# Loading x once, token-major, and turning it on the array, with low-rank products by token block

## The chip, the cores and the metric

One core of a Trainium2 chip runs the whole program. The metric is the device time of one execution in microseconds (us). The core has a matrix engine (PE, with its weight loads, PEld, shown apart), VectorE (DVE), ScalarE (ACT), GpSimd (POOL) and a queue engine (SP) that only issues DMAs here; ACT also issues some.

## The reference

A two-layer decoder trunk on 512 tokens of width 1024, all in float32. Layer 0 is an RWKV-7 time mix, layer 1 a differential attention; only the head of layer 0 matters here:

```python
xn = rms_norm(h, norm_pre[i])
x_prev = jnp.pad(xn, ((0, 0), (1, 0), (0, 0)))[:, :-1]
xmix = xn[None] + (x_prev - xn)[None] * mu[:, None, None, :]
rkvg = jnp.einsum('cbsd,cde->cbse', xmix[:4], w_in)
xw, xa = xmix[4], xmix[5]
w_pre = (w0 + jnp.tanh(xw @ w1) @ w2).astype(f32)
a = jax.nn.sigmoid((a0 + (xa @ a1) @ a2).astype(f32))
```

So x is normalised per token, multiplied by a gain per channel, and mixed with the token before it six times, with six vectors mu: four mixes go into products with 1024x1024 weights (r, k, v, g), two into low-rank products of width 64 (w1 and a1, side by side 128 columns).

## The kernel before

**Work and tiles.** Channels lie on the 128 partitions in 8 tiles (d = 0 to 7), tokens in 4 blocks of 128 (tb). A large product is split into high and low float32r parts and made of three matmuls of 512 columns (`mm3`, L284 to L287). `fill` (L909) walks the weight halves in the order r0, k0, v0, r1, k1, v1, ... (`ORDER`, L35); for each, `dense_m` (L396) needs for every d the split weight (`w_split`, L304) and the mixed activation (`mix`, `mixed`, L512 to L531), and then issues 4 x 3 matmuls.

**Order.** Each part of the work is a generator that yields its engine and an estimated cost. A planner (`Streams`, L45) runs them at build time: it always takes the step that can start earliest by its own clock, and among equals the one with the lower priority number. The instruction order of PE, DVE, ACT and POOL is the order in which the planner took the steps, and each engine runs its list in order. Buffers are counted: 4 PSUM banks for products (`pd`) and 4 for the rest (`pw`), 8 split weights (`WT`), 2 raw weights (`RAW`), 2 mixed tiles for even d and 2 for odd d (`MT`).

**The head.** `x_load` (L435) loads, on SP's queue and in this order: the vectors `vec`, the low-rank weights `w1a1`, two quarters of a channel-major copy of x (`xT`), the identity, the four token blocks of x, and the other two quarters of `xT`. All these pieces of x and `w1a1` have 512 KB. `x_in` (L462) squares a token block on ACT, takes the root on POOL (`rsqrt`, L275) and scales the identity with it (L474); `x_norm` (L477) turns the four diagonal matrices into one row of norms on every partition by four matmuls with ones (L492) and an ACT copy (L494). `lora_w` (L565) multiplies the low-rank weights with the mixing vectors, half on DVE and half on POOL (L573). `lora` (L580) makes the low-rank products of the still unnormalised x, 2 x 8 matmuls of 512 columns (L589, L590); `lora_out` (L595) multiplies both results with the norms (L600, L602) and adds them one token apart (L605). `x_scale` (L499) multiplies each channel tile with gain and norms (L504), and only then may `mixed` run on it: ACT L519, DVE L521, ACT L523 and DVE L525. The priorities are 0 for `x_load`, `x_in`, `lora_w` and `lora`, 6 for `x_scale`, 4 and 5 for the mixes, 7 for the weight splits, and 8 for `fill`. `w_split` waits until the norms are there. `r_evac` (L670) empties r's banks, and `decay` (L742) builds the decays from them and from the low-rank results (PE L749, L750).

Of the kernel before, what the change touches and what calls it, by code (L numbers as in the profile page):

```python
# [202 lines left out]
def yoco_kernel(ctx: ExitStack, tc: tile.TileContext, I, out):  # L203
# [58 lines left out]
    vec = cload("vec", [P, NVEC, NT])  # L262
# [41 lines left out]
    def w_split():  # L304
        yield "wait", ("norms",)
# [126 lines left out]
    xt, dg = [None] * NB, [None] * NB  # L432
    xh, norm, w1a1 = [], [], []

    def x_load():  # L435

        yield "DMA!", 0.2
        yield "set", ("vec",)
        for n in ("w", 0, 1, "x", 2, 3):
            if n == "w":  # L440
                yield "take", "R", 2
                w1a1.extend(R([P, NT, P]) for _ in range(2))
                yield "DMA!", 1.46
                nc.sync.dma_start(w1a1[0], I["w1a1"])
                yield "set", ("w1a1",)
            elif n == "x":
                yield "DMA!", 0.2
                nc.sync.dma_start(ident, I["ident"])
                for tb in range(NB):
                    yield "take", "R", 1  # L450
                    xt[tb] = R([P, D])
                    yield "DMA!", 1.46
                    nc.sync.dma_start(xt[tb], I["x"][tb])
                    yield "set", ("x", tb)
            else:
                yield "take", "R", 1
                xh.append(R([P, 2, S]))
                yield "DMA!", 1.46
                nc.sync.dma_start(xh[n], I["xT"][n])
                yield "set", ("xT", n)  # L460

    def x_in(tb):  # L462
        yield "wait", ("x", tb)
# [3 lines left out]
        yield "ACT", 1.04  # L467
        nc.scalar.activation(sq, xt[tb], AF.Square, accum_out=ss)
        yield "free", "R", 2
        r = yield from rsqrt(small, ss, 1.0 / D, EPS, 1, "rs")  # L470
        yield "take", "H", 1
        dg[tb] = HT([P, P])
        yield "DVE+", 0.15
        nc.vector.tensor_scalar(dg[tb], ident, r, None, ALU.mult)  # L474
        yield "set", ("dg", tb)

    def x_norm():  # L477

        ones = T(ax, [P, P], "ones")
        yield "Pool!", 0.1  # L480
        nc.gpsimd.memset(ones, 1.0)
        yield "take", "H", 1
        yield "take", "pw", 1
        nrm = bank("pw")
        n_ = HT([P, S])
        norm.append(n_)
        for tb in range(NB):
            yield "wait", ("dg", tb)
        yield "PE", 0.86
        for tb in range(NB):  # L490
            sl = slice(tb * P, (tb + 1) * P)
            nc.tensor.matmul(nrm[:, sl], ones, dg[tb], start=True, stop=True)  # L492
        yield "ACT", 0.52
        nc.scalar.copy(n_, nrm)  # L494
        yield "set", ("norms",)
        yield "free", "H", 4
        yield "free", "pw", 1

    def x_scale():  # L499
        yield "wait", ("norms",)  # L500
        for d in range(NT):
            yield "wait", ("low", d)
            yield "DVE+!", 0.66
            nc.vector.scalar_tensor_tensor(x_at(d), x_at(d), vcol(V_G, d), norm[0], ALU.mult, ALU.mult)  # L504
            yield "set", ("xh", d)
# [6 lines left out]
    def mixed(key, d, t):  # L512
# [8 lines left out]
        nc.vector.scalar_tensor_tensor(m[:, 1:], x_at(d)[:, 0 : S - 1], vcol(V_MU + c, d), m[:, 1:], ALU.mult, ALU.add)  # L521
# [58 lines left out]
    def lora():  # L580
# [4 lines left out]
        for d in range(NT):  # L585
            yield "wait", ("w1", d // 4)
            yield "wait", ("xT", d // 2)
            yield "PE", 1.71
            nc.tensor.matmul(ps, w1[:, d, :], x_at(d), start=(d == 0), stop=(d == NT - 1))  # L589
            nc.tensor.matmul(pm, m1[:, d, :], x_at(d), start=(d == 0), stop=(d == NT - 1))  # L590
            yield "set", ("low", d)
# [1392 lines left out]
```

## Time and profile before

| | |
|---|---|
| median of 3 runs | 792.98 us (791.94 to 794.04) |
| the profiled execution, its time | 797.09 us |
| the profiled execution, its span | 795.3 us |
| mean granted clock of PE over the span | 0.989 |
| instructions | 13941 |

The profile is that of one execution. A row of the timeline gives the start, the time that the merged instructions take together, engine, line, operation, written and read tile, a count, and in brackets the idle time before and what ended it. The end of a matmul is modelled and overlaps the next one's start, so the pace of PE is read from start to start. One f32 matmul of the low-rank products is two records.

### The profile page before, as it was taken

What the parts mean: (1) busy time and instruction counts of PE and PEld (TensorE: products, weight loads), DVE (VectorE), ACT (ScalarE), POOL (GpSimd) and SP (SyncE); (2) the same over time, 40 slices, a digit from 0 to 9 for tenths busy, and PEclk for the clock granted to TensorE, in tenths of its full rate; (3) what the DMA queues carried; (4) which work ended last, traced back from release to release, by engine and by line L of the source; (5) the groups of instructions that cost most, each with busy time, mean ns of one, the idle gap of its engine ahead of it and who ended that gap; (6) DMA issues with size and microseconds to landing.
All of it is one profiled execution on the core that took longest, in us unless ns stands there. A gap on an engine that the chain in (4) does not pass through costs nothing.

```text
span 795.3 us, 13941 instructions
## 1 busy us (share of the span) xinstructions
PE 756.1 (95%) x5016; PEld 605.1 (76%) x5016; DVE 589.8 (74%) x1360; ACT 454.5 (57%) x1078; POOL 201.9 (25%) x221
## 2 busy tenths in 40 slices
PE   6899999998999899999989999999999999999996
PEld 3576578875777677777778888887888888888884
DVE  2989999976798898998676685446874768835844
ACT  3779745688875446664444564333764566743431
POOL 2416615521451425666010010000000001100000
PEclk9999999998999899999999999999999999999998
DMA  8585669843684687463446444488943523314602
GB/s 325 197 285 196 245 225 290 298 147 105 209 286 171 217 301 258 145 228 105 133 166 247 133 146 135 172 309 226 312 158 92 159 53 121 117 43 159 259 6 106
DMA packets 66677, 148.79 MB, mean 187 GB/s; under 512 B 6576, under 2 KB 27312, under 8 KB 66608
## 3 DMA queue, kind: packets, MB, share of 16 engines
q1 hardware_dynamic: 43824, 112.25, 41.9%
q10 hardware_dynamic: 22784, 35.66, 13.1%
q8 instruction: 39, 0.64, 0.3%
q14 instruction: 30, 0.25, 0.1%
HBM read 110.13 MB, written 37.75 MB: 186 GB/s over the span
## 4 chain that ended last, share of the span: by engine, by line
PE 70%; DVE 8%; ACT 8%; DMA 8%; issue 2%; POOL 2%; SPq 1%; ACTq 0%; POOLq 0%; DVEq 0%
PE p L285 18%; PE p L287 18%; PE p L286 18%; PE p L1788 2%; PE p L984 2%; PE p L1188 2%; ACT R L270 1%; PE p L1753 1%; PE p L1752 1%; PE p L1201 1%; DMA R<-bD 1%; PE p L1779 1%; DMA RAW<-in_ple_w 1%; PE p L1410 1%; DMA R<-mD 1%
## 5 line engine op out<-in xcount | busy, mean ns | idle before, releaser
L285 PE MATMUL p<-R,R 128*128 128x512 f32 x800 | 326.4, 408 | 3.2 <-DVE R L270 1.7
L286 PE MATMUL p<-R,R 128*128 128x512 f32 x800 | 314.1, 393 | 3.8 <-DVE R L525 3.6
L287 PE MATMUL p<-R,R 128*128 128x512 f32 x800 | 314.4, 393 | 0.0
L285 PEld LDWEIGHTS p<-R,R 128*128 128x128 f32 x800 | 151.3, 189 | 37.1 <-DVE R L270 1.9
L287 PEld LDWEIGHTS p<-R,R 128*128 128x128 f32 x800 | 151.0, 189 | 33.2 <-DVE R L1318 0.4
L286 PEld LDWEIGHTS p<-R,R 128*128 128x128 f32 x800 | 151.5, 189 | 32.4 <-DVE R L525 4.9
L318 POOL TENSOR_TENSOR R<-RAW,R 128x512 fp32r<-128x512 f32 x59 | 78.6, 1339 | 163.3 <-ACT R L270 89.1
L270 ACT CAST R<-RAW 128x512 fp32r<-128x512 f32 x110 | 66.1, 619 | 26.7 <-DMA RAW<-in_w_g 10.0
L318 DVE TENSOR_TENSOR R<-RAW,R 128x512 fp32r<-128x512 f32 x81 | 56.8, 715 | 11.0 <-ACT R L270 10.2
L324 DVE SCALAR_TENSOR_TENSOR R<-RAW,vec,R 128x512 fp32r<-128x512 f32 x64 | 46.6, 748 | 13.9 <-ACT R L322 13.7
L322 ACT ACTIVATE R<-RAW,vec 128x512 fp32r<-128x512 f32 x64 | 44.6, 720 | 17.0 <-DMA RAW<-in_b_w_in 9.1
L1397 POOL TENSOR_TENSOR hr<-hm,half 128x1 f32<-128x1 f32 x16 | 10.4, 648 | 147.2 <-DVE hm L1395 147.2
L1757 DVE CUSTOM_DVE_ANT_0 p<-p,cmask 128x128 f32<-128x128 f32 (+3 forms) x64 | 30.3, 509 | 17.4 <-PE p L1753 17.3
L1764 ACT ACTIVATE H<-p,mx 128x128 f32<-128x128 f32 (+3 forms) x64 | 33.3, 526 | 15.7 <-DVE mx L1761 14.1
L281 POOL TENSOR_TENSOR orr<-orm,half 128x4 f32<-128x4 f32 x8 | 8.4, 1055 | 123.3 <-DVE orm L279 93.3
L1054 DVE TENSOR_TENSOR p<-p,H 128x126 f32<-128x126 f32 (+22 forms) x124 | 32.6, 263 | 4.3
L1051 DVE TENSOR_TENSOR H<-p,R 128x126 f32<-128x126 f32 (+22 forms) x124 | 30.5, 246 | 1.1
L1534 DVE SCALAR_TENSOR_TENSOR R<-H,R 128x512 f32<-128x512 f32 x16 | 11.1, 691 | 24.5 <-ACT H L1527 23.1
L1527 ACT ACTIVATE H<-p 128x512 f32<-128x512 f32 x16 | 9.5, 596 | 31.6 <-PE p L287 31.6
L521 DVE SCALAR_TENSOR_TENSOR p<-R,vec,p 128x511 f32<-128x511 f32 x32 | 23.5, 747 | 5.4 <-ACT p L519 5.3
L519 ACT ACTIVATE p<-R,omm 128x512 f32<-128x512 f32 x32 | 22.0, 695 | 5.0 <-DVE R L525 3.7
L1788 PEld LDWEIGHTS p<-R,H 128*128 128x128 f32 x160 | 22.1, 191 | 2.8 <-ACT H L1805 0.5
(227 smaller groups left out, 1249.4 us busy)
## 6 DMA issues: line engine op xcount, KB each, us to landing
R<-mD SPq DMA_DIRECT2D x40, 512.0 KB, 5.3
mD<-R ACTq DMA_DIRECT2D x32, 512.0 KB, 4.3
RAW<-in_ple_gate SPq DMA_DIRECT2D x16, 512.0 KB, 3.7
RAW<-in_kv_w SPq DMA_DIRECT2D x16, 512.0 KB, 3.9
RAW<-in_b_w_in SPq DMA_DIRECT2D x16, 512.0 KB, 3.9
R<-bD ACTq DMA_DIRECT2D x24, 256.0 KB, 5.2
R<-in_x SPq DMA_DIRECT2D x8, 512.0 KB, 6.8
RAW<-in_w_r SPq DMA_DIRECT2D x8, 512.0 KB, 4.0
```

The costliest lines, as they stand in the source:

```text
L270: (nc.scalar.copy if sc.eng == "ACT" else ENG[sc.eng].tensor_copy)(dst, src)
L285: nc.tensor.matmul(ps, ah, bh, start=first, stop=False)
L286: nc.tensor.matmul(ps, ah, bl, start=False, stop=False)
L287: nc.tensor.matmul(ps, al, bh, start=False, stop=last)
L318: ENG[sc.eng].tensor_sub(lo, f, hi.bitcast(F32))
L322: nc.scalar.activation(hi, f, AF.Copy, scale=g)
L324: nc.vector.scalar_tensor_tensor(lo, f, g, hi.bitcast(F32), ALU.mult, ALU.subtract)
L1051: ve.tensor_mul(tmp[:, 0:m, 0:w], bc(xs[:, s_ : s_ + 1, 0:w], [P, m, w]), bc(nb[:, s_ + 1 : 32, s_ : s_ + 1], [P, m, w]))
L1054: ve.tensor_add(xs[:, s_ + 1 : 32, 0:w], xs[:, s_ + 1 : 32, 0:w], tmp[:, 0:m, 0:w])
L1757: nc.vector.tensor_tensor_reduce(scs[m][:, 0:n], scs[m][:, 0:n], cmask[:, S - n : S], 1.0, -3.0e38, ALU.add, ALU.max, mx[:, m : m + 1])
L1764: nc.scalar.activation(E[m][:, 0:n], scs[m][:, 0:n], AF.Exp, bias=mx[:, m : m + 1], scale=0.125, accum_out=sm[:, m : m + 1])
L1788: nc.tensor.matmul(po[:, x * P : (x + 1) * P], aT[:, kb * P : (kb + 1) * P], vT[hg, kb // 2][:, kb % 2, x * P : (x + 1) * P], start=(kb == 0),
```

## The change

The channel-major copy of x is no longer an input. The four token blocks are loaded first, `w1a1` behind the first of them, and `vec` and the identity are issued on ACT's queue. Each block is squared, its root taken, and the block itself scaled (128x1024, DVE); then 8 transposes on PE turn it into two PSUM banks, and four copies on ACT or DVE write the channel-major tiles. The norm matmuls (`x_norm`) and `x_scale` are gone; the gain is folded into the mixing coefficients (`omm`, and a new `gmu`). `lora` runs by token block, 4 x 8 pairs of matmuls of 128 columns, each as soon as its block is turned, with priority 6 where it had 0; `lora_out` no longer multiplies with the norms. `w_split` waits for the last block to be scaled.

```diff
     def w_split():
-        yield "wait", ("norms",)
+        yield "wait", ("normed", NB - 1)
...
     def x_load():
 
-        yield "DMA!", 0.2
-        yield "set", ("vec",)
-        for n in ("w", 0, 1, "x", 2, 3):
-            if n == "w":
+        for t, n in ((vec, "vec"), (ident, "ident")):
+            nc.scalar.dma_start(t, I[n])
+            yield "set", (n,)
+        yield "take", "R", 4
+        xh.extend(R([P, 2, S]) for _ in range(4))
+        for tb in range(NB):
+            yield "take", "R", 1
+            xt[tb] = R([P, D])
+            yield "DMA!", 1.46
+            nc.sync.dma_start(xt[tb], I["x"][tb])
+            yield "set", ("x", tb)
+            if tb == 0:
                 yield "take", "R", 2
                 w1a1.extend(R([P, NT, P]) for _ in range(2))
                 yield "DMA!", 1.46
                 nc.sync.dma_start(w1a1[0], I["w1a1"])
                 yield "set", ("w1a1",)
...
     def x_in(tb):
...
         nc.scalar.activation(sq, xt[tb], AF.Square, accum_out=ss)
-        yield "free", "R", 2
+        yield "free", "R", 1
         r = yield from rsqrt(small, ss, 1.0 / D, EPS, 1, "rs")
-        yield "take", "H", 1
-        dg[tb] = HT([P, P])
-        yield "DVE+", 0.15
-        nc.vector.tensor_scalar(dg[tb], ident, r, None, ALU.mult)
-        yield "set", ("dg", tb)
...
+        yield "DVE+", 0.66
+        nc.vector.tensor_scalar(xt[tb], xt[tb], r, None, ALU.mult)
+        yield "set", ("normed", tb)
+        yield "wait", ("ident",)
+        for g in range(2):
+            yield "take", "pw", 1
+            pt = bank("pw")
+            yield "PE", 0.45
+            for x in range(4):
+                d = 4 * g + x
+                nc.tensor.transpose(pt[:, x * P : (x + 1) * P], xt[tb][:, d * P : (d + 1) * P], ident)
+            for u in range(2):
+                yield "ACT/DVE", (0.32, 0.35)
+                copy(xh[2 * g + u][:, :, tb * P : (tb + 1) * P], pt[:, 2 * u * P : 2 * (u + 1) * P].rearrange("p (a b) -> p a b", b=P))
+                yield "set", ("xb", tb, 2 * g + u)
+            yield "free", "pw", 1
+        yield "free", "R", 1
+
+    def x_ready():
         for d in range(NT):
-            yield "wait", ("low", d)
-            yield "DVE+!", 0.66
-            nc.vector.scalar_tensor_tensor(x_at(d), x_at(d), vcol(V_G, d), norm[0], ALU.mult, ALU.mult)
+            for tb in range(NB):
+                yield "wait", ("xb", tb, d // 2)
             yield "set", ("xh", d)
...
-        nc.vector.scalar_tensor_tensor(m[:, 1:], x_at(d)[:, 0 : S - 1], vcol(V_MU + c, d), m[:, 1:], ALU.mult, ALU.add)
+        nc.vector.scalar_tensor_tensor(m[:, 1:], x_at(d)[:, 0 : S - 1], gmu[:, c, d : d + 1], m[:, 1:], ALU.mult, ALU.add)
...
-        for d in range(NT):
-            yield "wait", ("w1", d // 4)
-            yield "wait", ("xT", d // 2)
-            yield "PE", 1.71
-            nc.tensor.matmul(ps, w1[:, d, :], x_at(d), start=(d == 0), stop=(d == NT - 1))
-            nc.tensor.matmul(pm, m1[:, d, :], x_at(d), start=(d == 0), stop=(d == NT - 1))
-            yield "set", ("low", d)
+        for tb in range(NB):
+            tsl = slice(tb * P, (tb + 1) * P)
+            for d in range(NT):
+                yield "wait", ("w1", d // 4)
+                yield "wait", ("xb", tb, d // 2)
+                yield "PE", 0.44
+                for t, w in ((ps, w1), (pm, m1)):
+                    nc.tensor.matmul(t[:, tsl], w[:, d, :], x_at(d)[:, tsl], start=(d == 0), stop=(d == NT - 1))
...
     def lora_out(ps, pm):
-        yield "wait", ("norms",)
-        yield "take", "H", 2
-        t, u = HT([P, S]), HT([P, S])
-        yield "DVE!", 0.66
-        nc.vector.tensor_mul(t, ps, norm[0])
+        yield "take", "H", 1
+        t = HT([P, S])
+        yield "ACT", 0.52
+        nc.scalar.copy(t, ps)
         yield "DVE", 0.66
-        nc.vector.tensor_mul(u, pm, norm[0])
+        nc.vector.tensor_add(t[:, 1:], t[:, 1:], pm[:, 0 : S - 1])
         yield "free", "pw", 2
-        yield "DVE+", 0.6
-        nc.vector.tensor_add(t[:, 1:], t[:, 1:], u[:, 0 : S - 1])
-        yield "free", "H", 2
...
-    sc.add(lora(), 0)
+    sc.add(lora(), XLP[0])
     sc.add(derive(), 0)
-    sc.add(x_norm(), -1)
-    sc.add(x_scale(), XLP[0])
+    sc.add(x_ready(), 0)
```

## Rows read from the trace of the kernel before

**Rows 1.** The page, busy time by engine.
```profile
PE 756.1 (95%) x5016; PEld 605.1 (76%) x5016; DVE 589.8 (74%) x1360; ACT 454.5 (57%) x1078; POOL 201.9 (25%) x221
```
**Rows 2.** Busy time by stretch: length, PE, PEld, DVE, ACT, POOL, PEclk, DMA, GB/s.
```profile
10.00:15.00 5.00, 5.00 (x10) 2.08 (x9) 1.76 (x8) 3.51 (x7) 2.18 (x4) 1.00 1.02 419
...
20.00:25.00 5.00, 5.00 (x12) 1.91 (x11) 4.79 (x6) 3.55 (x7) 2.34 (x2) 1.00 0.00 0
...
60.00:80.00 20.00, 18.15 (x77) 13.52 (x76) 18.64 (x31) 19.90 (x39) 14.19 (x13) 1.00 0.52 194
...
100.00:120.00 20.00, 20.00 (x130) 15.69 (x130) 18.32 (x47) 9.53 (x21) 2.84 (x3) 1.00 0.62 222
```
**Rows 3.** The timeline of PE up to the first large product.
```profile
7.16 2.07 PE L589 MATMUL p<-R,R 128*128 128x512 f32 x2 [7.16 <-DVE R L573]
...
10.73 1.91 PE L589 MATMUL p<-R,R 128*128 128x512 f32 x2
...
12.44 1.07 PE L590 MATMUL p<-R,R 128*128 128x512 f32 x2
...
18.50 1.05 PE L492 MATMUL p<-H,ones 128*128 128x128 f32 x8
...
19.39 1.02 PE L589 MATMUL p<-R,R 128*128 128x512 f32 x2
...
22.82 1.02 PE L589 MATMUL p<-R,R 128*128 128x512 f32 x2
...
23.68 1.02 PE L590 MATMUL p<-R,R 128*128 128x512 f32 x2
...
24.63 0.51 PE L285 MATMUL p<-R,R 128*128 128x512 f32 x1
```
**Rows 4.** The timeline of loads, norms and scaling in the same stretch.
```profile
1.17 0.42 SPq L444 DMA_DIRECT2D R<-in_w1a  x1
...
4.96 2.14 DVE L573 TENSOR_TENSOR R<-R,mug 128x512 f32<-128x512 f32 x2 [1.38 <-DMA R<-in_w1a]
...
5.08 2.92 POOL L573 TENSOR_TENSOR R<-R,mug 128x512 f32<-128x512 f32 x2 [4.10 <-DMA R<-in_w1a]
...
8.91 1.06 ACT L468 ACTIVATE R<-R 128x1024 f32<-128x1024 f32 x1 [6.91 <-DMA R<-in_x]
...
10.91 0.29 DVE L474 TENSOR_SCALAR H<-ident,rsr 128x128 f32<-128x128 f32 x1 [0.66 <-POOL rsr L281]
...
20.21 3.09 DVE L504 SCALAR_TENSOR_TENSOR R<-R,vec,H 128x512 f32<-128x512 f32 x3 [5.24 <-ACT H L494]
```
**Rows 5.** Groups of lines by shape: busy, mean ns of one, idle before.
```profile
L504 DVE SCALAR_TENSOR_TENSOR R<-R,vec,H 128x512 f32<-128x512 f32 x8 | 8.4, 1065 | 5.2 <-ACT H L494 5.2
...
L519 ACT ACTIVATE p<-R,omm 128x512 f32<-128x512 f32 x32 | 22.0, 695 | 5.0 <-DVE R L525 3.7 <-DVE R L504 1.3
...
L1561 DVE TENSOR_SCALAR R<-R,rsr 128x1024 f32<-128x1024 f32 x4 | 3.0, 747 | 0.0
...
L1441 ACT CAST R<-p 128x256 fp32r<-128x256 f32 x16 | 5.9, 368 | 6.9 <-PE p L1436 4.4 <-DVE R L1443 2.5
```
**Rows 6.** The timeline of PE: eight transposes between large products.
```profile
88.89 1.04 PE L893 MATMUL p<-ident,H 128*128 128x128 f32 x8
89.68 0.47 PE L285 MATMUL p<-R,R 128*128 128x512 f32 x1
```
**Rows 7.** Groups of PE's lines between 24.6 and 90 us, with idle time before them.
```profile
L286 PE MATMUL p<-R,R 128*128 128x512 f32 x70 | 27.7, 395 | 3.6 <-DVE R L525 3.6
...
L749 PE MATMUL p<-R,R 128*128 128x512 f32 x8 | 3.5, 440 | 1.6 <-DVE R L800 0.7 <-ACT R L674 0.6 <-DVE R L525 0.3
...
L893 PE MATMUL p<-ident,H 128*128 128x128 f32 x16 | 2.2, 280 | 1.3 <-ACT H L888 1.3
```
**Rows 8.** The timeline of PE: eight sums over heads, late and in time.
```profile
79.32 2.78 PE L824 MATMUL p<-H,hsel 128*32 128x512 f32 x8
...
95.97 1.06 PE L824 MATMUL p<-H,hsel 128*32 128x512 f32 x8
```

More of the change, by code (lines that the diff above doesn't have):

```diff
@@ L260, in late_loads @@
             nc.sync.dma_start(t, src)
-    vec = cload("vec", [P, NVEC, NT])
+    vec = T(cp, [P, NVEC, NT], "vec")
     ident = T(cp, [P, P], "ident")
@@ L430, in yoco_kernel @@
             want_t(key, I["w_" + key], (hf,))
-    xt, dg = [None] * NB, [None] * NB
-    xh, norm, w1a1 = [], [], []
+    xt = [None] * NB
+    xh, w1a1 = [], []
     def x_load():
-        yield "DMA!", 0.2
-        yield "set", ("vec",)
-        for n in ("w", 0, 1, "x", 2, 3):
-            if n == "w":
+        for t, n in ((vec, "vec"), (ident, "ident")):
[10 more added lines that the diff above has]
+            if tb == 0:
                 yield "take", "R", 2
@@ L445, in x_load @@
                 yield "set", ("w1a1",)
[L446 to L460, printed above, removed]
     def x_in(tb):
@@ L466, in x_in @@
         ss = T(small, [P, 1], "ss")
-        yield "ACT", 1.04
+        yield "ACT", 1.24
         nc.scalar.activation(sq, xt[tb], AF.Square, accum_out=ss)
-        yield "free", "R", 2
+        yield "free", "R", 1
         r = yield from rsqrt(small, ss, 1.0 / D, EPS, 1, "rs")
-        yield "take", "H", 1
-        dg[tb] = HT([P, P])
-        yield "DVE+", 0.15
-        nc.vector.tensor_scalar(dg[tb], ident, r, None, ALU.mult)
-        yield "set", ("dg", tb)
[L477 to L499, printed above, removed]
-        yield "wait", ("norms",)
+        yield "DVE+", 0.66
[16 more added lines that the diff above has]
+    def x_ready():
         for d in range(NT):
-            yield "wait", ("low", d)
-            yield "DVE+!", 0.66
-            nc.vector.scalar_tensor_tensor(x_at(d), x_at(d), vcol(V_G, d), norm[0], ALU.mult, ALU.mult)
+            for tb in range(NB):
+                yield "wait", ("xb", tb, d // 2)
             yield "set", ("xh", d)
@@ L595, in lora_out @@
     def lora_out(ps, pm):
-        yield "wait", ("norms",)
-        yield "take", "H", 2
-        t, u = HT([P, S]), HT([P, S])
-        yield "DVE!", 0.66
-        nc.vector.tensor_mul(t, ps, norm[0])
+        yield "take", "H", 1
+        t = HT([P, S])
+        yield "ACT", 0.52
+        nc.scalar.copy(t, ps)
         yield "DVE", 0.66
-        nc.vector.tensor_mul(u, pm, norm[0])
+        nc.vector.tensor_add(t[:, 1:], t[:, 1:], pm[:, 0 : S - 1])
         yield "free", "pw", 2
-        yield "DVE+", 0.6
-        nc.vector.tensor_add(t[:, 1:], t[:, 1:], u[:, 0 : S - 1])
-        yield "free", "H", 2
         yield "ACT", 0.52
@@ L695, in yoco_kernel @@
     der = T(ax, [P, 6, NT], "der")
-    omm = T(ax, [P, 4, NT], "omm")
+    omm, gmu = T(ax, [P, 4, NT], "omm"), T(ax, [P, 4, NT], "gmu")
     mug = T(ax, [P, 2, NT, 2], "mug")
@@ L708, in derive @@
         yield "set", ("mug",)
-        yield "DVE", 0.52
-        nc.vector.tensor_scalar(omm, vec[:, V_MU : V_MU + 4, :], -1.0, 1.0, ALU.mult, ALU.add)
+        yield "DVE+", 0.1
+        nc.vector.tensor_mul(gmu, vec[:, V_MU : V_MU + 4, :], bc(vec[:, V_G, :].unsqueeze(1), [P, 4, NT]))
+        yield "DVE+", 0.1
+        nc.vector.tensor_sub(omm, bc(vec[:, V_G, :].unsqueeze(1), [P, 4, NT]), gmu)
+        yield "DVE", 0.5
         nc.vector.tensor_scalar(der[:, 0, :], vec[:, V_W0, :], 0.5, None, ALU.mult)
@@ L1931, in _layout @@
     o["x"] = a["x"].reshape(NB, P, D)
-    o["xT"] = a["x"].reshape(S, 4, 2, P).transpose(1, 3, 2, 0)
     o["lnxg"] = a["a_lnx_g"][0]
```

## The prediction

> **What bounds the kernel now.** I read the busy time by engine first: PE is busy 95% of the span [rows 1], so a gain must come from idle PE time, from PE work at half pace, or from PE work that goes away. Then the stretches [rows 2]: between 100 and 120 us PE is busy for all 20 us, between 60 and 80 us it is not (18.15) while ACT is (19.90 of 20) and DVE nearly is (18.64). So the head of the kernel is set by PE's late start, then by ACT and DVE, and from about 90 us by PE again. What is won or lost before 90 us should be carried to the end, as long as the later order stays as good.
>
> The timeline of PE's head [rows 3] shows three things. PE idles until 7.16 us, waiting for DVE's product of w1a1 with the mixing vectors. Its first low-rank matmuls go at half pace: 10.73 to 12.44 is 1.71 us for one, 22.82 to 23.68 is 0.86 us. The granted clock of that stretch reads 1.00 all the same [rows 2], so I go by the pace: 1.2 GHz for the first 5.3 us after PE's first matmul, 2.4 GHz after. And the low-rank products end at 23.68 + 0.86 = 24.54 us, where the first large product starts, at 24.63.
>
> Why is the first mix no earlier? The norms pass through PE (18.50 us, behind low-rank products), ACT and eight scalings on DVE, which begin at 20.21 [rows 4] and cost 8.4 us in all [rows 5]; DVE is busy 4.79 of 5 us there [rows 2]. PE's large products then wait for L525, the last step of a mix: 3.6 us in three waits, besides 1.6 us before L749 and 1.3 us before L893 [rows 7]. Each wait costs some 0.25 us more from start to start than is listed as idle, which for eight waits is an estimated 2 us. One burst of L824 takes 2.78 us where the same burst in time takes 1.06 [rows 8]: 1.7 us. Together PE loses 3.6 + 1.6 + 1.3 + 2.0 + 1.7 = 10.2 us between 24.6 and 90 us.
>
> **Loads.** Four 512 KB loads of xT go, 4 x 1.25 us at the 419 GB/s of the loading stretch [rows 2]. w1a1, issued at 1.17, was in use at 4.96 [rows 4]: 3.8 us. The first block of x, issued first at about 0.7, should be there at 4.5, w1a1 at 5.8, the other blocks at 7.0, 8.3 and 9.5 us. The two issues on ACT come before its table load and its first square; ACT has nothing else until 4.5 us, so they cost nothing; without that cover they would cost their two issue times, under 1 us.
>
> **Block 0 on DVE.** From the start of a square to DVE's next use of the root it is 2.0 us (8.91 to 10.91) [rows 4], so block 0 could be scaled at 6.5. But DVE has two products of w1a1 ahead, 2.14 us because POOL runs beside the second [rows 4]: 5.8 to 7.9. With 0.75 us for the scaling, the same operation as L1561 [rows 5], block 0 is scaled at 8.65. Blocks 1 to 3 follow behind the 16 copies (0.37 us each by the nearest row [rows 5], half of them on either engine) and are scaled by about 14 us. All mixes may start at about 15, where they start at 21 now.
>
> **PE before the first large product.** Eight transposes take 88.89 to 89.68, 0.10 us each at full pace [rows 6], so 32 take 3.2 us. A f32 matmul of 128 columns takes (19.39 - 18.50) / 4 = 0.22 us [rows 3], so 64 take 14.2 us, against 16 x 0.86 = 13.8 before. The four norm matmuls (0.9 us) go. PE has 17.4 us of work at full pace instead of 14.7, and it starts at 8.65 instead of 7.16. I take the half pace to last 5.3 us from the first work, as before, thus until 13.95, with 0.5 us of gaps between transposes and products: 2.4 us of work is done by then, and the rest ends at 13.95 + 15.0 = 29.0 us. The low-rank products stay ahead of the first large product, since the planner gives PE to priority 6 before 8 whenever both are ready. So the first large product starts at 29.0 instead of 24.6: 4.4 us later. Bounds: at full pace throughout, 26.1; with half pace up to 20.8 (the slower rival), 32.4.
>
> The rows show no transposes at the beginning of PE's work, so they don't tell whether these count towards the rise. The Trainium skill ("TensorE: Matmul & The Clock Gate", Part 4: PE-mode transpose) says that they don't count as PE being busy in the same way. By that the 5.3 us would begin with the first product at about 10.4, and the sum would be 0.8 us later; no row here speaks against it.
>
> **What comes back.** ACT and DVE have from 15 to 29 us to work ahead: four mixed tiles and eight split weights, all that the buffers hold. Before, the first product found one mix ready. So the waits for L525 should go: 3.6 + 0.3 us [rows 7] and 1.0 us of restarts. The low-rank results come 4 us later, but the decays that use them start only with r's evacuation near 50 us, so that is covered; if it were not, L749 would wait longer. The wait for r's evacuation (0.6) I count as half gone with the lead on ACT. In all 5.2 us. What I take to stay are the waits for L800 and L888 and the late burst of L824, about 5 us, because they hang on chains behind r's and k's evacuations, which ACT and DVE run as before, and because PE's order is written by a planner that reckons ACT shorter than it is (a mix's first step 0.57 us, measured 0.695 [rows 5]). The small steps (gmu, the tanh input as an ACT copy, one DVE product less) lie on DVE and ACT while PE has 29 us of its own work: nothing. If that cover were gone they would cost under 1 us.
>
> **Sum.** +4.4 - 5.2 = -0.8 us. The profiled execution took 797.09 us with a span of 795.3; it would take 796.3. The median of the runs is 792.98, 4.1 us below the profiled one, so the forecast is 792.2 us: no change that can be told. About 0.3%, 2.4 us, is what a measurement of this kernel can tell from no change.
>
> **Rivals.** Faster: the lead of ACT and DVE also carries the chains behind the evacuations. For it: 60 to 80 us is an ACT stretch [rows 2], four mixes and eight splits ahead are some 9 us of ACT, and DVE is rid of 8.4 us of scaling. Then all but 0.8 of the 10.2 us comes back: +4.4 - 9.4 = -5.0, 788.0 us. Against it: those chains begin at the end of r0, which is no earlier than before.
>
> Slower: the array stays at half pace while the blocks come in. For it: PE starts with transposes and pieces of 128 columns with copies in between, not with an unbroken run of 512. The transposes of the last block end at about 15.5; if the 5.3 us only begin there, half pace lasts to 20.8. Then (20.8 - 8.65 - 0.5) / 2 = 5.8 us of work is done, 11.6 remain, and the first large product starts at 32.4: +7.8 - 5.2 = +2.6, 795.6 us; with the other waits as long as now or the gaps larger, up to 797. It decides from a first large product later than 32.2 us. The rule on transposes quoted above works in this direction.
>
> The change is not a null one by construction: the loads, scalings and norm matmuls named in it must vanish from the trace. But the waits may all stay except the two before 31 us (2.9 us): +4.4 - 2.9 = +1.5, 794.5, still no change that can be told; I count it with the forecast.
>
> **How the numbers follow.** The forecast with its variant, 792.2 to 794.5, gets 0.38; the faster rival 0.35; the slower 0.27. The last two are as high because the planner orders all later work anew, which can make or take away a stall of 2 or 3 us anywhere. The range reaches from 786.5, the faster rival with such a stall less, to 797.0, the slower one with its gaps; about 2 in 10 lies outside. The likeliest case alone has 790.0 to 795.0.
>
> **What would show it.** In the changed profile: the first L468 near 4.5 us, the last block scaled near 14, transposes from about 8.7; the pace of the low-rank matmuls doubling near 14; the first L285 near 29; hardly any wait of L286 for L525 before 60 us; waits before the sums over heads and L893 still there. A first L285 before 26 or after 32.2, or waits of L749 as long as 1.6 us gone altogether, would prove a step wrong; so would a gain or loss that appears only after 100 us.

## The result, and the profile after

The changed kernel took 799.70 us (median of 20 executions, 796.48 to 801.67). The kernel before, in 20 executions taken beside them on the same chip, took 796.63 us (791.94 to 801.43); the 792.98 us at the head of this document are the median of the first three of these. The ratio is 1.0044, with a 95% interval of 1.0029 to 1.0059: the change made the kernel slower by about 3.5 us. The forecast was no change that can be told; the sign it left at 0.27 came out. The profiled execution took 800.39 us, with a span of 798.6 us and a mean granted clock of 0.987.

The page's busy times of the changed kernel answer to [rows 1].
```profile
PE 761.2 (95%) x5136; PEld 621.5 (78%) x5136; DVE 592.9 (74%) x1373; ACT 457.2 (57%) x1087; POOL 181.1 (23%) x205
```
PE has 5.1 us more of busy time, POOL 20.8 us less; the other shares stand as they were. Shares of the whole span tell little here. The stretches tell more; they answer to [rows 2], with the same columns, and one stretch is added, 80 to 90 us.
```profile
20.00:25.00 5.00, 5.00 (x47) 5.00 (x46) 4.66 (x8) 4.18 (x8) 1.28 (x1) 1.00 0.74 231
...
60.00:80.00 20.00, 19.97 (x86) 15.10 (x85) 19.02 (x33) 19.78 (x39) 7.92 (x9) 1.00 0.61 223
80.00:90.00 10.00, 7.57 (x39) 4.62 (x36) 10.00 (x22) 6.24 (x13) 8.36 (x7) 1.00 0.38 129
```
The added stretch in the kernel before:
```profile
80.00:90.00 10.00, 8.61 (x44) 5.41 (x44) 10.00 (x20) 8.18 (x15) 7.81 (x7) 1.00 0.68 247
```
Between 60 and 80 us PE lost 1.85 us before and loses 0.03 now. But from 80 to 90 us PE is busy for only 7.57 of 10 us (8.61 before). DVE has no idle moment there in either kernel: a lead of PE runs into it.

The timeline of loads and first steps in the changed kernel answers to [rows 4].
```profile
0.73 0.39 SPq L446 DMA_DIRECT2D R<-in_x  x1
0.74 0.41 ACTq L438 DMA_DIRECT2D vec<-in_vec  x1
...
4.95 1.06 ACT L462 ACTIVATE R<-R 128x1024 f32<-128x1024 f32 x1 [2.00 <-DMA R<-in_x]
5.11 0.17 DVE L684 TENSOR_TENSOR mug<-vec 128x16 f32<-128x16 f32 x1 [5.11 <-DMA vec<-in_vec]
...
6.34 1.42 DVE L555 TENSOR_TENSOR R<-R,mug 128x512 f32<-128x512 f32 x2
...
7.40 1.25 POOL L555 TENSOR_TENSOR R<-R,mug 128x512 f32<-128x512 f32 x1
...
7.67 1.53 DVE L466 TENSOR_SCALAR R<-R,rsr 128x1024 f32<-128x1024 f32 x1
...
10.81 0.75 DVE L466 TENSOR_SCALAR R<-R,rsr 128x1024 f32<-128x1024 f32 x1
```
Block 0 is squared at 4.95 us, DVE's two products of w1a1 start at 6.34, and the block is scaled from 7.67 to 9.20. The scaling of block 0 takes 1.53 us, that of block 1 only 0.75: POOL's product of 7.40 to 8.65 runs beside the first.

PE's timeline answers to [rows 3] and [rows 6].
```profile
9.26 1.11 PE L475 MATMUL p<-ident,R 128*128 128x128 f32 x4 [9.26 <-DVE rsm L279]
10.89 1.22 PE L574 MATMUL p<-R,R 128*128 128x128 f32 x4 [0.52 <-DVE rsm L279]
...
14.47 1.91 PE L475 MATMUL p<-ident,R 128*128 128x128 f32 x8
16.17 1.10 PE L574 MATMUL p<-R,R 128*128 128x128 f32 x8
17.11 0.60 PE L475 MATMUL p<-ident,R 128*128 128x128 f32 x4
...
19.31 11.78 PE L574 MATMUL p<-R,R 128*128 128x128 f32 x104
30.84 0.48 PE L285 MATMUL p<-R,R 128*128 128x512 f32 x1
```
Read from start to start: eight transposes take 1.70 us at 14.47 (0.21 each) and four take 0.44 at 17.11 (0.11 each), so the clock goes from 1.2 to 2.4 GHz at about 16.2 us; the trace's own clock record has the rise at 16.26. From 19.31 to 30.84 us there are 104 records of two per product: 0.222 us for one product. The transposes begin at 9.26 us and the first large product starts at 30.84, 6.2 us later than before.

The groups of PE's lines between 24.6 and 90 us answer to [rows 7] (the low-rank result is used at L731 now, and the key's columns are turned at L875).
```profile
L286 PE MATMUL p<-R,R 128*128 128x512 f32 x68 | 26.5, 389 | 0.0
...
L731 PE MATMUL p<-R,R 128*128 128x512 f32 x8 | 3.2, 395 | 0.0
...
L875 PE MATMUL p<-ident,H 128*128 128x128 f32 x16 | 2.4, 281 | 1.6 <-ACT H L870 1.4
...
L965 PE MATMUL p<-R,R 64*128 64x128 f32 x2 | 0.5, 308 | 0.6 <-DVE R L716 0.6
```
All 3.6 us of waits for a mix are gone, and so are the 1.6 us before the decays. What is left comes after 78 us, as PE's timeline there shows; it answers to [rows 8].
```profile
78.41 2.77 PE L806 MATMUL p<-H,hsel 128*32 128x512 f32 x8
81.11 0.50 PE L285 MATMUL p<-R,R 128*128 128x512 f32 x1
...
85.34 1.18 PE L875 MATMUL p<-ident,H 128*128 128x128 f32 x8 [1.44 <-ACT H L870]
...
89.43 0.46 PE L965 MATMUL p<-R,R 64*128 64x128 f32 x2 [0.63 <-DVE R L716]
```
The sums over heads are as late as before (2.77 us for a burst that takes 1.06 in time), and the key chain on ACT and DVE then holds PE up at L875 and at the gram products L965. ACT's step L870, for which L875 waits, had itself waited for DVE:
```profile
84.67 2.17 ACT L870 COPY H<-c 128x512 f32<-128x512 f32 x4 [2.10 <-DVE c L827]
```

**Where the time went.** To compare two kernels at a point in time I added up, for each trace, the matmuls not yet started, each at its spacing at 2.4 GHz (0.227 us for 512 columns of a large product, and so on). From 31 us on both have the same work to come, so the difference is how far the changed kernel is behind. From 200 us on, where many small matmuls run, an entry can be off by about 1 us, as their spacing is less certain; the last entry is the difference of the spans.

| at (us) | 40 | 70 | 90 | 140 | 180 | 200 | 240 | 295 | 320 | 350 | 410 | end |
|---|---|---|---|---|---|---|---|---|---|---|---|---|
| behind by (us) | +3.2 | -1.0 | +1.0 | +1.6 | +1.8 | -1.7 | +2.4 | +1.1 | +6.8 | +9.1 | +4.0 | +3.3 |

It starts 6.2 us behind, is 1.0 us ahead at 70 us, and has lost 2.6 us again by 140. The rest comes long after the change, where the recurrence runs among the large products: 8 us are lost between 295 and 350 us and 5 won back by 410. There the orders differ: leaving the heads out, PE's list of matmuls, read by line, is the same in both traces up to 49 us and again from 411 us on, and differs in many places between. That called for experiments of two kinds: on the head, and on the order after it.

### The profile page after: what moved, and what is told of

Same layout as the page of the kernel before. It is cut to its first block, busy times and chain, and to the rows that moved or that the text cites. A ratio compares the mean times of both kernels' runs of the same rounds, so it can differ in the third digit from the quotient of the medians.

```text
span 798.6 us, 14188 instructions
## 1 busy us (share of the span) xinstructions
PE 761.2 (95%) x5136; PEld 621.5 (78%) x5136; DVE 592.9 (74%) x1373; ACT 457.2 (57%) x1087; POOL 181.1 (23%) x205
## 4 chain that ended last, share of the span: by engine, by line
PE 51%; DVE 3%; DMA 2%; issue 1%; ACT 1%; POOL 0%; ACTq 0%; DVEq 0%; POOLq 0%
PE p L287 14%; PE p L285 14%; PE p L286 14%; PE p L1769 2%; PE p L1734 1%; PE p L1733 1%; PE p L1760 1%; DMA R<-bD 1%; PE p L1391 1%; DMA RAW<-in_b_w_in 1%; PE p L1169 0%; PE p L1417 0%; PE p L1808 0%; ACT R L322 0%; DVE R L318 0%
## 5 line engine op out<-in xcount | busy, mean ns | idle before, releaser
L318 POOL TENSOR_TENSOR R<-RAW,R 128x512 fp32r<-128x512 f32 x48 | 63.3, 1328 | 172.8 <-ACT R L270 95.2
L318 DVE TENSOR_TENSOR R<-RAW,R 128x512 fp32r<-128x512 f32 x92 | 63.9, 707 | 16.3 <-ACT R L270 15.5
L1437 ACT COPY R<-p 128x512 f32<-128x512 f32 x16 | 9.4, 588 | 29.8 <-PE p L287 29.7
L505 ACT CAST R<-p 128x512 fp32r<-128x512 f32 x32 | 18.2, 585 | 14.0 <-DVE p L503 13.8
L503 DVE SCALAR_TENSOR_TENSOR p<-R,gmu,p 128x511 f32<-128x511 f32 x32 | 23.6, 746 | 2.1 <-ACT p L501 2.1
```

The lines of the kernel that those rows point to most:

```text
L318: ENG[sc.eng].tensor_sub(lo, f, hi.bitcast(F32))
```

## The experiments

Each kernel was timed beside the kernel before on the same chip, unless said otherwise. The ratios, and where the first large product started in the profiled execution:

| edit | kernel | ratio to before, 95% | first large product (us) |
|---|---|---|---|
| old order from 130 us on | changed | 1.0038 (1.0016 to 1.0060) | 29.57 |
| the same again | changed | 1.0024 (1.0002 to 1.0045) | 29.89 |
| nothing, again | changed | 1.0058 (1.0037 to 1.0079) | 31.25 |
| new order from 130 us on | before | 1.0090 (1.0057 to 1.0124) | 25.04 |
| bias 0.14 | before | 1.0144 (1.0118 to 1.0170) | 24.66 |
| bias 0.14 | changed | 1.0134 (1.0111 to 1.0156) | 30.08 |
| bias 0.16 | before | 1.0023 (1.0005 to 1.0041) | 23.98 |
| bias 0.16 | changed | 1.0129 (1.0108 to 1.0151) | 29.79 |
| constants back on SP | changed | 1.0076 (1.0046 to 1.0105) | 30.31 |
| low-rank products behind | changed | 1.0314 (1.0278 to 1.0351) | 22.98 |
| low-rank products whole | changed | one execution, 797.41 us | 31.23 |
| 27 warming matmuls | before | 0.9983 (0.9966 to 1.0000) | 23.54 |
| 44 warming matmuls | changed | 1.0113 (1.0092 to 1.0133) | 32.71 |
| 16 warming matmuls | before | 0.9968 (0.9953 to 0.9982) | 22.09 |
| 21 warming matmuls | changed | 1.0041 (1.0022 to 1.0059) | 29.38 |

**The head alone, and the order alone.** The planner was made to take, from 130 us of its own clock on, the steps of all streams but the head's in the order that it had written for the other kernel. So the changed head runs with the old later order, and the old head with the new one. By line, PE's lists in the traces agree with that: each replay has the other kernel's list from 132 or 138 us on.
```diff
...
+            if self.rest is None and t >= FROM:
+                n, self.rest = dict(self.done), []
+                for nm, e in self.kept:
+                    if n.get(nm, 0) > 0:
+                        n[nm] -= 1
+                    else:
+                        self.rest.append((nm, e))
+                self.rest.reverse()
...
```

> The changed head, and from 130 us of the planner's clock on the order that the planner chose for the kernel before (each step that is still to come, in that kernel's order). Theory (the head costs 1 to 1.5 us, read at 140 us as the matrix work that is still to come; the rest of the 3.5 us is the planner's other order between 230 and 410 us, with two more stretches at half clock): +1 to +1.5 us, ratio about 1.0015, and no stretch at half clock between 290 and 320 us. Rival (the head's later start alone costs it): +3.5 us, ratio 1.0044, whatever the later order.

> The converse: the head of the kernel before, and from 130 us on the order that the planner chose for the changed kernel. Theory: +2 to +2.5 us against the kernel before, ratio about 1.003, with stretches at half clock between 290 and 320 us. Rival (it is the head): no difference, ratio 1.000.

The changed head with the old order took 798.48 us against 795.32, and the old head with the new order 802.03. The first ratio, 1.0038, is nearer the rival's 1.0044 than the theory's 1.0015; the second, 1.0090, goes beyond the theory's 1.003 and leaves its rival out. So the new order is worse by itself, at least behind a head that it was not written for, and the new head costs something by itself. The stretch from 290 to 350 us shows what the order does. The kernel before:
```profile
290.00:320.00 30.00, 27.63 (x479) 21.67 (x478) 27.43 (x69) 20.02 (x57) 14.63 (x17) 1.00 0.74 253
320.00:350.00 30.00, 29.97 (x286) 23.95 (x286) 29.03 (x52) 19.81 (x53) 21.55 (x22) 1.00 0.57 190
```
The changed kernel, same view:
```profile
290.00:320.00 30.00, 25.91 (x410) 20.42 (x410) 27.28 (x67) 17.08 (x46) 12.66 (x13) 0.83 0.79 262
320.00:350.00 30.00, 27.96 (x284) 22.06 (x283) 26.23 (x47) 21.00 (x60) 18.94 (x22) 1.00 0.35 118
```
The changed head with the old order, same view:
```profile
290.00:320.00 30.00, 27.68 (x464) 21.48 (x464) 27.36 (x68) 19.45 (x56) 14.64 (x17) 0.94 0.82 271
320.00:350.00 30.00, 29.96 (x284) 24.22 (x280) 28.89 (x51) 19.02 (x51) 20.74 (x21) 1.00 0.57 182
```
With the old order PE is busy for 57.6 of the 60 us under either head. In the changed kernel it is 53.9, and its granted clock from 290 to 320 us is 0.83, a mean of stretches at 2.4 and at 1.2 GHz. The theory's "no stretch at half clock" held only in part (0.94). The loss of this stretch belongs to the order: the old head with the new order reads 25.59 and 27.98 us busy there, as the changed kernel does. It is not all lost for good: of the 9.1 us that the changed kernel is behind at 350 us, 4.0 are left at 410.

The replay was run again, beside the changed kernel itself, to narrow the split.

> The kernel of e1 once more (new head, later order of the kernel before), to narrow its interval of 1.0016 to 1.0060, on one chip with the changed kernel (e14). Theory (the head is worth 1.4 us, the mean of the matrix work still to come at 140 us over five profiles with the new head less three with the old; the rest of the 3.5 us is the later order): pooled ratio near 1.002, and 1.5 to 2.5 us faster than e14. Rival (the head costs all of it, part of it only after 140 us): the same as e14 within 0.7 us.

> The changed kernel itself, for comparison with e13 on the same chip: ratio 1.003 to 1.006. Theory: 1.5 to 2.5 us above e13. Rival: level with e13. Its profile adds one more reading of the clock's rise (13.8 to 16.3 us so far) and of the work still to come at 140 us (608.2 to 609.4 so far).

Replay 797.80, changed kernel 801.39, kernel before 796.60 us: on this chip the replay is 3.6 us faster than the changed kernel, more than the theory's 1.5 to 2.5, and against the rival (level within 0.7 us). Over both measurements the gap is smaller. The mean of the two replays is a ratio of 1.0031, some 2.5 us; the mean of the two measurements of the changed kernel is 1.0051, some 4.1 us. So roughly 2.5 us go with the head and 1.6 with the later order. The intervals overlap, and the split is a reading, not a measurement. Single traces scatter as much: by matmuls to come, the two replays are 0.5 and 1.1 us behind the kernel before at 140 us, and their spans are 0.1 and 3.3 us longer. Of the second's 3.3 us, 1.6 come between 410 and 450 us, where its clock was at 1.2 GHz from 410.4 to 413.8 us and the first's was not.

**The order disturbed on purpose.** `PREF` is the bias by which the planner prefers one engine to another where a step may run on either. A step of 0.01 us changes no work, only the order and the sharing out. The lists of PE, DVE, ACT and POOL, read by line, stay as they were up to 105 us or later in all four of these runs, so the head is not touched.
```diff
-PREF = 0.15
+PREF = 0.14
```

> The kernel before with one constant of the planner moved from 0.15 to 0.14 us (its preference between engines where a step may go to either); the work is the same, the orders differ in some 400 lines of PE's list. Theory (the kernel's constants were fitted to one order, and any other order of the same work costs a few us, whatever causes it): 2 to 6 us slower than before, ratio 1.002 to 1.008. Rival (the planner's order is worth nothing by itself): the same within 1 us.

> The changed kernel with the same constant moved from 0.15 to 0.14. Theory (its order is one of many, not fitted): between 2 us faster and 3 us slower than the changed kernel, ratio to the kernel before 1.002 to 1.008, no worse than the kernel before under the same move. Rival (the new head costs 3.5 us by itself, on top of any order): 3 us or more slower than the kernel before under the same move.

And with 0.16:

> As e7, the planner's constant at 0.16 instead of 0.14, kernel before. Theory (the constants were fitted to one order): slower again, ratio 1.003 to 1.015, with the loss between 160 and 420 us, where the recurrence runs between the large products. Rival (e7 was one bad order): within 1.002.

> As e8, the constant at 0.16, changed kernel. Theory (the head costs 1 us, the rest is the order): within 4 us of the kernel before under the same move (e11), either sign, and matrix work still to come at 140 us 0.5 to 1.5 us more than there. Rival (the new head costs 3.5 us on top of any order): 3 us or more slower than e11.

The kernel before took 806.97 us with 0.14 and 796.96 with 0.16, the changed one 806.36 and 806.47. The plan alone, order and sharing out, is thus worth up to 1.4%, three times the effect that was to be predicted. The theories did only half well: with 0.14 the new head is no worse than the old, as forecast, but both ratios are beyond the forecast 1.008; with 0.16 the kernel before hardly loses, and the changed one is 9.5 us slower than it, which the rival (3 us or more) had right. Of these 9.5 us, 2.0 are there at 140 us; most of the rest comes after 200 us, so the order has to do with it, and not the head alone. New head against old head is +0.44% at 0.15, -0.10% at 0.14 and +1.06% at 0.16. No one of these is "the" effect of the change. The stretch from 290 us shows where the kernel before loses with 0.14:
```profile
290.00:320.00 30.00, 21.16 (x245) 15.69 (x246) 28.58 (x72) 14.14 (x34) 13.41 (x14) 0.83 0.72 239
320.00:350.00 30.00, 29.89 (x426) 24.25 (x427) 26.61 (x50) 20.40 (x60) 15.11 (x16) 1.00 0.39 127
```
PE is busy for 51.05 of 60 us, and the 30 us from 290 hold 245 matmuls in place of 479: fewer of the recurrence's small ones are done by then. The head of this kernel is not behind; at 140 us it has 607.6 us of matrix work to come, the kernel before 607.8.

These runs give a second measure of the head. Matrix work still to come at 140 us is 607.8, 607.6, 606.9 and 608.2 us in the four traces with the old head, and 609.4, 608.2, 608.9, 608.5, 608.9, 608.9 and 609.6 in seven with the new one: means of 607.6 and 608.9. The changed head puts PE 1.3 us behind.

**Constants back on SP's queue.** The two loads go ahead of x on SP's queue, as `vec` did before; the orders on PE, DVE and POOL are those of the changed kernel.
```diff
-            nc.scalar.dma_start(t, I[n])
+            nc.sync.dma_start(t, I[n])
```

> The changed kernel, but vec and the identity are issued on SP's queue ahead of x, as before; the planner's order is the same as in the changed kernel. Theory (vec lands at 5.1 instead of 2.7 us beside the first block of x, so eight small steps of DVE and the products of w1a1 stand in front of the scaling of block 0): the derived vectors start near 2.7, block 0 is scaled about 0.5 to 1 us earlier, the first large product starts 0.3 to 1 us earlier than 30.84, and the time falls by as much. Rival (constants on another queue are harmless, x is later by their issue): the first large product 0.5 us later.

The timeline of this run:
```profile
2.65 0.18 DVE L684 TENSOR_TENSOR mug<-vec 128x16 f32<-128x16 f32 x1 [2.65 <-DMA vec<-in_vec]
...
5.66 1.06 ACT L462 ACTIVATE R<-R 128x1024 f32<-128x1024 f32 x1 [3.66 <-DMA R<-in_x]
...
8.30 1.53 DVE L466 TENSOR_SCALAR R<-R,rsr 128x1024 f32<-128x1024 f32 x1
```
`vec` is there at 2.65 us where it came at 5.11, and that helps nobody: the theory missed. Block 0 is there 0.71 us later, and everything behind it is 0.63 us later. In the changed kernel DVE's steps on `vec` just fit in ahead of the root's first step (6.18 us). So the second queue is worth about 0.6 us, and the late `vec` costs next to nothing. Yet this run's first large product came at 30.31, half a microsecond before that of the changed kernel's profile, because its clock rose at about 14.5 us and not at 16.3. The time, 801.22 us, can't be told from the changed kernel's by their intervals.

**Low-rank products behind the large ones.** If their 14 us at the start are the cost, they could be spread out:
```diff
-    sc.add(lora(), XLP[0])
+    sc.add(lora(), 9)
```

> The changed kernel with the low-rank products at priority 9, behind the large products at 8: PE takes them only where the large products wait. Theory (PE is bound by its work from 13 us on, so the order of that work changes nothing before 78 us): the first large product starts near 22 to 24, but r0 with the low-rank products together ends at the same time, within 0.5 us, and the total stays within 2 us of the changed kernel. Rival (the late first large product is what costs): the chains behind r's evacuation start some 6 us earlier and the time falls by 3 us or more.

Theory and rival both missed: 819.81 us, 3.1% slower. The groups of PE between 24.6 and 110 us say why:
```profile
L731 PE MATMUL p<-R,R 128*128 128x512 f32 x8 | 5.3, 663 | 6.1 <-DVE R L617 5.3 <-ACT H L748 0.8
```
The decays' matmuls wait 5.3 us for L617, the split of the second low-rank weights. These are loaded only when the low-rank results are there (`lora2` waits for `lora`), so a late product brings a late load and a late split with it. PE does start its first large product at 22.98 us here, but being late for the decays costs more than the 8 us in question. The wait is only the first part of it: from 80 to 100 us PE is busy for 12.20 of 20 us at a granted clock of 0.66, and at 140 us this run is 14 us behind the changed kernel by matmuls to come. That the products stay first is right.

**Low-rank products whole.** They run over 512 columns after the last block is turned.
```diff
-        for tb in range(NB):
...
-                yield "wait", ("xb", tb, d // 2)
-                yield "PE", 0.44
...
+        for d in range(NT):
+            yield "wait", ("w1", d // 4)
+            yield "wait", ("xh", d)
+            yield "PE", 1.71
...
```

> The changed kernel with the low-rank products of 512 columns over all four blocks at once, after the last block is turned (one part undone; the planner orders all else anew). Read up to 140 us alone. Theory (by block, products fill PE while blocks come in): PE idles between the transposes until about 16 us, the first large product starts near 33 to 35 instead of 30.8, and 2 to 4 us more matrix work is still to come at 60 us. Rival (pieces of 128 columns and their weight loads cost more than they fill): first large product at 31 or sooner.

PE's timeline of this run, from its first product on (at L572 here):
```profile
16.20 2.71 PE L572 MATMUL p<-R,R 128*128 128x512 f32 x4
...
31.23 0.80 PE L285 MATMUL p<-R,R 128*128 128x512 f32 x1
```
All but the last eight transposes pass at 1.2 GHz, with gaps between; the products run from 16.20, all but the first at 2.4 GHz (the clock record has the rise at 17.72), and the first large product starts at 31.23 us. The rival was nearer. Products by block start 5.3 us sooner and gain 0.4 us against this one execution: what they do early they do at half pace, between gaps. Against the mean of six such heads (30.2 us, below) it would be 1.0 us.

**Half pace, taken out of either head.** PE is idle for its first 7 to 9 us. Matmuls of ones into a bank whose content is overwritten afterwards fill that time; the planner does not know of them, so the order is unchanged, and PE's lists in the traces are the same but for them. In the kernel before (the tile of ones is also filled earlier, at the program's start):
```diff
...
+        for _ in range(27):
+            nc.tensor.matmul(ps[:, 0:P], ones, ones, start=True, stop=True)
...
```

> The kernel before, with 27 matmuls of 128 columns of ones put ahead of PE's first low-rank product, where PE idles (their result is overwritten); the planner doesn't count them, so all orders stay as they were. Theory (half pace in the head is paid in full while PE's head sets the first norms): the low-rank matmuls go 0.86 us apart from the first on, the first large product starts near 22.5 instead of 24.6, and the time falls by 1 to 2.5 us, ratio 0.997 to 0.999. Rival (between 25 and 90 us ACT and DVE set the pace, and PE only waits longer): first large product earlier, time the same within 0.7 us.

> The changed kernel with 44 such matmuls ahead of PE's first transpose, the planner's orders unchanged. Theory: the half pace from 9.3 to 14 or 16 us is worth 2.4 to 3.5 us of PE's head, the first large product starts near 27.5 to 28.5 instead of 30.8, nothing but PE's work bounds the stretch up to 78 us, and about 1 to 3 us of it reach the end: ratio to the kernel before 1.001 to 1.003 instead of 1.0044. Rival (DVE's chain between 79 and 91 us is what ends last in the head): the first large product is earlier, the first L965 still comes at 89 us, and the ratio stays at 1.004.

I had mis-sized one such matmul: it is two records, 0.215 us at full pace. The 27 ran to 8.8 us and the 44, put ahead of the changed kernel's first transposes, to 12.9, both past the point where real work was ready. The kernel before gained 0.17% in spite of it, with an interval that reaches to none. The changed kernel became slower still: its first large product came 1.9 us later than without, and its trace is 1.6 us further behind at 140 us and ends 2.3 us later (a span of 800.9 us against 798.6). By the ratios the end is some 5.5 us later (1.0113 less 1.0044), but the profiled execution was this run's fastest. What makes up the remainder was not traced.

With fewer of them (16 and 21):

> As e5, with 16 matmuls of ones instead of 27, whose last ones stood in the way of the first low-rank product: they ended at 8.6 us, where that product could start at 7.2. Theory (PE's half pace and its first products set the head of the kernel before): the first large product 1.0 to 1.4 us earlier than in e5, matrix work still to come at 140 us 1 us less than in e5, ratio 0.996 to 0.998. Rival (nothing more to gain, ACT and DVE set the pace): as e5, 0.998.

> As e6, with 21 matmuls of ones instead of 44: those of e6 ended at 12.6 us and delayed the first transposes by 3.3 us. Theory (the same orders, only PE's head sooner): first transposes at 9.3 us at full pace, first large product near 28, work still to come at 140 us 1 us less than in the changed kernel, ratio 1.001 to 1.004, and clearly under e6's 1.011. Rival (where later steps meet is chance, and a head that is sooner by 2 us is as likely to lose by it): ratio anywhere from 1.000 to 1.010.

PE's timeline of the kernel before with 16:
```profile
1.03 5.64 PE L586 MATMUL p<-ones 128*128 128x128 f32 x32 [1.03 <-POOL ones L267]
7.26 1.12 PE L591 MATMUL p<-R,R 128*128 128x512 f32 x2 [0.59 <-DVE R L573]
8.22 1.02 PE L592 MATMUL p<-R,R 128*128 128x512 f32 x2
...
22.09 0.49 PE L287 MATMUL p<-R,R 128*128 128x512 f32 x1
```
Its first real product takes 0.96 us where one took 1.71 at that time before [rows 3]; the first large product starts 2.5 us sooner, and the kernel takes 792.58 us against 795.32: a ratio of 0.9968 (0.9953 to 0.9982), as its theory had it. This version beats both kernels. By matmuls to come its trace is ahead of the kernel before by 2.5 us at 31 us, 2.0 at 140 and 2.7 at 700: with the orders held, what the head won stayed won. PE's timeline of the changed kernel with 21:
```profile
1.03 6.29 PE L476 MATMUL p<-ones 128*128 128x128 f32 x42 [1.03 <-POOL ones L267]
9.18 0.66 PE L480 MATMUL p<-ident,R 128*128 128x128 f32 x4 [1.86 <-DVE rsm L281]
10.35 0.93 PE L579 MATMUL p<-R,R 128*128 128x128 f32 x4 [0.52 <-DVE rsm L281]
11.08 1.92 PE L480 MATMUL p<-ident,R 128*128 128x128 f32 x8
...
29.38 0.48 PE L287 MATMUL p<-R,R 128*128 128x512 f32 x1
```
and its stretch from 10 to 15 us:
```profile
10.00:15.00 5.00, 4.65 (x27) 4.65 (x28) 4.04 (x9) 3.20 (x9) 2.77 (x3) 0.66 0.67 244
```
The four transposes at 9.18 go at full pace, the eight at 11.08 at half: the clock fell again, after PE had been idle from 7.3 to 9.2 and then had four transposes. Here the first large product is 1.5 us earlier than in the changed kernel, at 29.38 where near 28 was forecast, and 0.5 us is left of that at 140 us; the time, 797.78 us (1.0041), can't be told from the changed kernel's.

## Why the prediction was wrong

**The base.** The forecast was set on 792.98 us, a median of three executions; twenty beside the changed kernel give 796.63. So 3.7 of the 7.5 us between the forecast 792.2 and the measured 799.70 are the base, and only the rest is the change. As a difference, the forecast was -0.8 us, in its likeliest case -3.0 to +2.0; measured are +3.1 by the medians and +3.5 by the ratio, past the +2.6 of the slower rival.

**The change did what it says.** Loads, scaling and norm matmuls went as described, and `vec` and the identity on ACT's queue cost nothing there.

**Block 0 on DVE: 9.20 us where 8.65 was forecast.** The first square started at 4.95 in place of 4.5, and with it the root's first step and the products of w1a1 (6.34 in place of 5.8). The contention between DVE and POOL was forecast for the products (2.14) and came upon the scaling (1.53): 1.42 + 1.53 = 2.95 us where 2.14 + 0.75 = 2.89 was reckoned. Sum right, place wrong.

**The first large product: 30.84 us where 29.0 was forecast.** PE starts 0.6 us later; the clock rises at about 16.2 us in place of 13.95, which is 2.3 us at half pace more, or 1.1 us of work. Transposes (0.11) and products (0.222) were sized right. The result lies within the bounds (26.1 to 32.4) and short of the slower rival's 32.2. But the rise is no fixed term: by the traces' clock records it came at 13.8, 14.3, 14.5, 14.9 and 16.9 us in five other runs with this head, 4.8 to 7.4 us after PE's first work over the six, and the first large product between 29.57 and 31.25. In four runs with the old head the rise came 3.8 to 5.8 us after PE's first work; the 5.3 us of the prediction were one draw from that. The mean of the first large product over the six is 30.2, against 24.6 over the four with the old head: 5.7 us later, where 4.4 was forecast. By the rule that the prediction quoted from the Trainium skill ("TensorE: Matmul & The Clock Gate", Part 4: PE-mode transpose: transposes do not count as PE being busy in the same way) it would have been 29.8. The fall at 10.7 us in the run with 21 warming matmuls agrees with it, though an idle stretch lies there too. The run with whole products is against it: nothing but transposes until 16.20 us, and the rise only 1.5 us behind the first product, where in the six it is 3.1 to 5.8 us behind. A scatter of 3 us under one head is more than the 0.8 us between the rule and the forecast, so the runs don't decide.

**What comes back: right in kind, too small, and then partly lost.** The waits for mixes went, as forecast. The lead was shorter than reckoned: the last block's transposes go between low-rank products and end at 19.31 us, and ACT's first step of a mix (L501) starts at 19.78, not at about 15; that cost nothing, as PE had low-rank work until 30.84. (Two readings of the kernel before were off by little: the waits listed are seven, not eight, and the first large product had only half a mix, since its second matmul waited 1.31 us for L525.) Besides, the waits of the decays (1.6 us) went altogether, which the prediction had named as a proof that a step was wrong: the lead on ACT and DVE did carry into the chains behind the evacuations, as the faster rival had it. By 70 us PE had made up 7.2 us, not 5.2, and was ahead. Then DVE, full from 80 to 90 us, took 2.0 of these back, and 0.6 more went by 140. The return was 4.6 us at 140 us, 0.6 less than forecast; the start 6.2 us later, 1.8 more. Net of the head: +1.6 us in this trace, +1.3 in the means of eleven traces, where the sum said -0.8.

**The steps that failed** are two. The first is the term +4.4 us for the first large product: it was +6.2 in this trace and +5.7 in the means, because the half pace was put at a fixed 5.3 us from PE's first work and lasted 7.0 here, and because PE started 0.6 us later. The return of 5.2, mis-sized by less, was 4.6. So the head costs 1.3 to 1.6 us by 140 us, where it was to win 0.8.

The second is the condition in "should be carried to the end, as long as the later order stays as good". The sum puts the order at nothing, and the order did not stay. The prediction did say that the planner orders all later work anew and can make or take away a stall of 2 or 3 us; it put that into the chances but not into the sum. With the old order held, the changed head costs some 2.5 us; its own order adds some 1.6 us, 3.6 on the chip where both ran. A change of bias that means nothing moves the kernel before by up to 1.4%, 11 us, and the changed one by 0.9%. That a head's gain is carried while the order holds was right, by the run with 16 warming matmuls.

Between the 2.5 us of the replays and the 1.3 us at 140 us lie 1.2 us without a place; the replays' intervals (from 0.2 to 4.8 us) are wide enough to hold them.

**The slower rival** had the right sign for partly the right reason: the half pace lasted longer. It did not last to 20.8 us, and its threshold, a first large product after 32.2 us, was not reached. What it lacked was the order, so that its +2.6 us comes near the measured difference is in part luck.

What stays open: how the 3.5 us divide exactly between head and order, since the intervals overlap; and which of the three biases gives the "true" sign of the change, for which three settings are too few.

## What to carry to other kernels

Where one engine is busy 95% of the span, work put on it at the start (here 2.7 us more at full pace, and 20 of the 32 transposes ran at half) must be paid back by waits that vanish, and one should look at which engine is full next: here DVE, ten microseconds after PE's waits had gone. Where a planner writes the instruction order, a change of under 1% can't be judged from one plan: hold the later order fixed, or compare over several harmless settings, before crediting or blaming the edit. A base of three executions can itself lie some us off. And a matrix engine that idles before its first work can be kept running on a tile of ones, if that ends before the work is ready and nothing idles behind it: that was worth 0.3% in the kernel before, and nothing that can be told in the changed one.

## What the hardware showed that was not expected

- The clock's rise under one and the same head varied between 13.8 and 16.9 us from run to run. With 21 warming matmuls it fell again at 10.7 us, after an idle stretch of 1.9 us, four transposes and a gap of 0.5 us.
- Later falls go with the order of the work: from 290 to 320 us PEclk reads 0.83 to 0.89 in all six profiles with the changed kernel's later order, under either head, and 0.94 to 1.00 in the five with the old one. Others belong to the execution: the changed kernel's profile has falls at 238 and 269 us that its second profile has not. Whether PE's idle time or the fall comes first was not taken apart.
- `vec`, issued at 0.74 us on ACT's queue beside block 0 on SP's, was in use only at 5.11 us, 0.16 us after the 512 KB block itself; alone at the head of SP's queue it was in use at 2.65.
- A scaling of 128x1024 on DVE takes 1.53 us with a POOL product beside it for most of its length and 0.75 without; the pair of w1a1 products, 2.14 us beside POOL's product before, takes 1.42 with that product beside it only from 7.40 us on, its last 0.36 us.
